# The MLP's first product by seven block products instead of eight, with weight sums made by DMA

## Chip, cores, metric

The kernel runs on one core of a Trainium2 chip, as one program and one launch. The metric is device time in microseconds of that program; lower is better. It was timed in 3 runs, and one more execution was taken with the profiler.

## What is computed

One decoder layer on 512 tokens of width 1024 in f32: retention with 8 heads, native sparse attention with 16 heads, a gated merge of both, an MLP with a squared ReLU, and a gated per-layer embedding. The part that the change touches most:

```
x  = x + (g_ret * o_ret + g_nsa * o_nsa) @ w_out[i]
h2 = rms_norm(x, norm_mlp_g[i])
x  = x + jnp.square(jax.nn.relu(h2 @ w_mlp_up[i])) @ w_mlp_down[i]        # 1024 -> 4096 -> 1024
x  = x + (p[i] @ w_ple_proj[i]) * jax.nn.sigmoid(rms_norm(x, norm_ple_g[i]) @ w_ple_gate[i])
return rms_norm(x, norm_final_g)
```

## The kernel before

Activations lie with features on the 128 partitions and the 512 tokens along the row; a tile is 128 x 512. Every f32 product is made of three matmuls (`mm3`, L254): each operand is split into a rounded part `hi` and a rest `lo`, and hi x hi, hi x lo and lo x hi are added in PSUM. Weights come from DRAM in pieces of 128 x 1024 (512 KB, class `Piece`) on SP's queue, into three buffers `raw`. ScalarE makes `hi` (L206) and VectorE `lo` (L209) of each half of a piece; there are rings of four such halves. In a matmul row of the profile, `ps_s<-gx_hi,hi 128x512` has the moving operand first and the stationary one after it.

The order of work is a list of items, `items`, that `run` (L223) walks through. An item has TensorE's part, a `post` step that takes the result from PSUM, and the weight halves that it needs; behind TensorE's part `run` lists the splits of up to three halves ahead, then what earlier steps put off with `defer`, then `post`. Each engine works through its own instructions in this order, and waits where an operand is not there.

Stages in order of time: norm and the narrow projections; eight retention heads, where the dense projections of head h are listed between the core of head h - 1 (`head_core`, L794; `mixed`, L892), with the output projection `ret_out` (L874) after every second head; sparse attention; the merge; `w_out`; the MLP; the embedding gate; the final norm.

- A head's core ends in a group norm. VectorE makes statistics, POOL runs a chain of 11 small operations for the inverse root (`rsqrt` with `eng=pool`, L302 to L298, result `rs_y`; VectorE for the last head), VectorE scales (`on`, L846), TensorE transposes (L857), VectorE gates.
- The MLP goes in two halves of 16 tiles of 128 hidden features. `up` (L1337) makes one tile: 8 blocks of 128 along the contraction, 24 matmuls of 512 columns, moving `gx`, the gained x. Its `post` multiplies by the norm's factor `rb1`, takes the ReLU, squares it and splits it into `hh` and `hl`. `down` (L1350) adds the second product of that half to `x1`.
- `gained` (L1306) makes `gx_hi` and `gx_lo` and sums squares for the next norm; `token_rstd` and `over_partitions` make the factor and spread it.
- `finish`, `deliver` and `finished` (L1414 to L1487) make the last norm by blocks of 128 tokens: gate with a tanh, add, square with a sum, gain on POOL, inverse root (POOL for two blocks, VectorE for two), multiply, store on SP.

Of the kernel before, what the change touches and what calls it, by code (L numbers as in the profile page):

```python
# [8 lines left out]
F32 = mybir.dt.float32  # L9
# [131 lines left out]
def _layer_kernel(ctx, tc, a, out):  # L141
# [35 lines left out]
    def issue(p):  # L177
        if p.keep:
            if p.raw is None:
                p.raw = P_[p.keep].tile([P, p.n], F32, name=f"raw_{p.keep}_{p.mark}")  # L180
                sp.dma_start(p.raw, p.src)
        elif p.raw is None:
# [3 lines left out]
            sp.dma_start(p.raw, p.src)  # L186
# [67 lines left out]
    def mm3(ps, sh, sl, mh, ml, first, last):  # L254

        pe.matmul(ps, sh, mh, start=first, stop=False)  # L256
        pe.matmul(ps, sh, ml, start=False, stop=False)  # L257
        pe.matmul(ps, sl, mh, start=False, stop=last)  # L258
# [77 lines left out]
    def token_rstd(accs, tag):  # L336


        def sums():
            ps = bank("t")  # L340
# [12 lines left out]
    def over_partitions(tag, dst):  # L353


        def go():
            T["bc"] = bank("t")
# [436 lines left out]
    def head_core(h):  # L794
# [76 lines left out]
        its.append(Item(0.9, turn, gated))  # L871
# [377 lines left out]
    def merge_start():  # L1249
        close("aw", "q", "kv")  # L1250
        T["nsa_p"] = []
        open_("np", bufs=1)
        open_("mp", bufs=1, side="right")
        open_("mw", bufs=2, side="right")
# [41 lines left out]
    def out_start():  # L1296
        close("mw", "np", "oret")
        xp = open_("xp", bufs=1)
        T["x1"] = [xp.tile([P, S], F32, name=f"x1_{n}") for n in range(KT)]
        T["gx"] = [(xp.tile([P, S], F32R, name=f"gx_hi{n}"), xp.tile([P, S], F32R, name=f"gx_lo{n}")) for n in range(KT)]  # L1300
        T["rb1"] = xp.tile([P, S], F32, name="rb1")
        open_("ew", bufs=2)
# [3 lines left out]
    def gained(n, g, acc):  # L1306

        hi, lo = T["gx"][n]
        x = T["x1"][n]
        gc = gains[:, g + n : g + n + 1]  # L1310
        act.activation(hi, x, AF.Copy, scale=gc)
        dve.scalar_tensor_tensor(lo, x, gc, hi.bitcast(F32), op0=ALU.mult, op1=ALU.subtract)
# [8 lines left out]
    for n in range(KT):  # L1321
# [5 lines left out]
        def post_x(ps, n=n):  # L1327
            dve.tensor_tensor(T["x1"][n], ps, T["xs", n], op=ALU.add)
            gained(n, G_MLP, "acc1")
# [4 lines left out]
    gxs = (lambda: T["gx"], KT)  # L1334
    hid = {}

    def up(hf, i):  # L1337
        def post(ps):
            t = P_["ew"].tile([P, S], F32, tag="t1", name="relu")
            dve.scalar_tensor_tensor(t, ps, 0.0, T["rb1"], op0=ALU.max, op1=ALU.mult)  # L1340
            hi = P_["hid"].tile([P, S], F32R, tag=f"hh{i}", name="hh")
            lo = P_["hid"].tile([P, S], F32R, tag=f"hl{i}", name="hl")
            act.activation(hi, t, AF.Square)  # L1343
            dve.tensor_tensor(t, t, t, op=ALU.mult)
            dve.tensor_tensor(lo, t, hi.bitcast(F32), op=ALU.subtract)
            hid[hf, i] = hi, lo

        return dense(("d", "v", "s", "s")[i % 4], [Piece(a["w_mlp_up"][16 * hf + i])], gxs, post)

    def down(hf, n):  # L1350
        def post(ps):
            x = T["x1"][n]
            dve.tensor_tensor(x, ps, x, op=ALU.add)
            if hf == 1:
                gained(n, G_PLE, "acc2")
# [3 lines left out]

    bc = over_partitions("n1", lambda: T["rb1"])  # L1360
    ups = [up(0, i) for i in range(16)]

    posts = []
    for u in ups[:2]:
        posts.append(u[-1].post)
        u[-1].post = None
    def mlp_start():
        close("mp", "th", "nf", "nx", "h")
        fp = open_("fp", bufs=1, side="right")
        T["ppf"] = fp.tile([P, NQ, D], F32, name="pp")  # L1370
# [12 lines left out]
    items += sum(ups[4:], [])
    items += sum((down(0, n) for n in range(KT)), [])
    add(Item(0, load_pp))
    items += sum((up(1, i) for i in range(16)), [])
    items += sum((down(1, n) for n in range(KT)), [])


    def ple_start():  # L1390
        close("hid")
        open_("fw", bufs=1, side="right")
# [5 lines left out]
    def turn_x(t, f2):  # L1398
# [7 lines left out]
        return Item(0.44, go, lambda: dve.tensor_tensor(T["x2t"][:, t, f], T["xt"], T["ppf"][:, t, f], op=ALU.add))  # L1406
# [7 lines left out]
    def finish(t, c0, c1, ps, col):  # L1414

        f = slice(c0, c1)
        x = lambda: T["x2t"][:, t, f]
# [6 lines left out]
        def take():  # L1424
            th = st["th"][:, : c1 - c0]
            dve.tensor_tensor(th, th, T["ppf"][:, t, f], op=ALU.mult)
            dve.tensor_tensor(x(), x(), th, op=ALU.add)

        def square():
            sq = P_["ew"].tile([P, S], F32, tag="sq", name="sq")  # L1430
            act.activation(sq[:, : c1 - c0], x(), AF.Square, accum_out=T["ss2"][:, t, col : col + 1])
            pool.tensor_tensor(x(), x(), T["gf"][:, f], op=ALU.mult)
# [3 lines left out]
    def deliver(t, cols):  # L1436
# [3 lines left out]
        def factors():  # L1440
# [5 lines left out]
            st["r"] = rsqrt(v, 1, "fn", pool if t < NQ - 2 else dve)  # L1446

        def scaled():
            r = st["r"]
            o = P_["fw"].tile([P, D], F32, tag="o", name="o", bufs=4)  # L1450
            act.activation(o[:, 0:S], T["x2t"][:, t, 0:S], AF.Copy, scale=r[:, 0:1])
            dve.tensor_scalar_mul(o[:, S:], T["x2t"][:, t, S:], r[:, 0:1])
# [176 lines left out]
```

## Time and profile before

| | us |
|---|---|
| median of 3 runs | 1268.94 (1268.21 to 1271.06) |
| the profiled execution | 1269.14 |
| its span | 1267.4 |
| TensorE busy | 1245.6 |
| VectorE busy | 770.9 |
| ScalarE busy | 528.8 |
| POOL busy | 213.4 |

The span is what the profile sees from its first to its last instruction; the execution's time is 1.7 us longer. Rows give a start in us, a duration in us, the engine (PE is TensorE, PEld its weight loads, DVE VectorE, ACT ScalarE, POOL GpSimd, SPq the queue that issues loads and stores), the line and the tiles, out<-in. Matmul rows overlap, since they are pipelined: the step from start to start is what one costs.

### The profile page before, as it was taken

The numbers are of one execution on the slowest core, as the hardware profiler recorded it, in microseconds if no ns is written. First come the engines' busy times: TensorE is split into PE (matmuls) and PEld (weight loads), VectorE is DVE, ScalarE is ACT, GpSimd is POOL, SyncE is SP. The second block draws the span as 40 slices with busy tenths as digits, with TensorE's granted clock in tenths as the row PEclk, the third lists the DMA queues.
The fourth block names the chain that finished last, engine by engine and source line by source line (L and its number), as shares of the span: only waits on it lengthen the run. The fifth ranks groups of instructions, "written<-read, shape, count | busy, mean of one in ns | idle before, by whom it ended". The sixth has DMA issues, their size and how long they took to land.

```text
span 1267.4 us, 16784 instructions
## 1 busy us (share of the span) xinstructions
PE 1245.6 (98%) x6312; PEld 1033.0 (82%) x6312; DVE 770.9 (61%) x1401; ACT 528.8 (42%) x1091; POOL 213.4 (17%) x290
## 2 busy tenths in 40 slices
PE   8999999999999999999999999999999999999996
PEld 6968898898998987788888888888888888888885
DVE  6766763665666587778878754555652345644456
ACT  5753333332332233677778642343322223323333
POOL 0040000000000023556574500000000000000045
PEclk9999999999999999999999999999999999999998
DMA  7532323223223222211010033332233342323221
GB/s 248 204 133 67 105 79 100 76 92 100 76 78 98 86 73 84 67 34 35 34 51 17 18 100 100 122 127 91 93 100 100 98 168 86 98 100 100 88 79 67
DMA packets 34513, 116.29 MB, mean 92 GB/s; under 512 B 4096, under 2 KB 4480, under 8 KB 34304
## 3 DMA queue, kind: packets, MB, share of 16 engines
q1 hardware_dynamic: 34432, 115.22, 27.8%
q8 instruction: 50, 0.82, 0.3%
q14 instruction: 31, 0.25, 0.1%
HBM read 111.01 MB, written 4.19 MB: 91 GB/s over the span
## 4 chain that ended last, share of the span: by engine, by line
PE 50%; DVE 2%; POOL 0%; ACT 0%; issue 0%; DVEq 0%; ACTq 0%
PE ps_s L256 6%; PE ps_s L257 6%; PE ps_s L258 6%; PE ps_d L256 4%; PE ps_d L258 4%; PE ps_d L257 4%; PE ps_v L256 3%; PE ps_v L257 3%; PE ps_v L258 3%; PE ps_t L1089 2%; PE ps_t L258 1%; PE ps_t L257 1%; PE ps_t L256 1%; PE ps_v L1106 1%; PE ps_v L1105 1%; PE ps_s L1014 1%
## 5 line engine op out<-in xcount | busy, mean ns | idle before, releaser
L206 ACT ACTIVATE hi<-raw 128x512 fp32r<-128x512 f32 (+1 forms) x364 | 222.7, 622 | 256.4 <-PE ps_v L258 60.5
L209 DVE TENSOR_TENSOR lo<-raw,hi 128x512 fp32r<-128x512 f32 (+1 forms) x350 | 242.5, 715 | 67.7 <-ACT hi L206 67.6
L209 POOL TENSOR_TENSOR lo_fw<-raw_fw,hi_fw 128x512 fp32r<-128x512 f32 x8 | 11.3, 1437 | 503.0 <-ACT hi_fw L206 503.0
L256 PE MATMUL ps_d<-h_hi,hi 128*128 128x512 f32 x216 | 89.6, 415 | 0.0
L258 PE MATMUL ps_d<-h_hi,lo 128*128 128x512 f32 x216 | 85.4, 395 | 0.0
L257 PE MATMUL ps_d<-h_lo,hi 128*128 128x512 f32 x216 | 85.3, 395 | 0.0
L1067 POOL TENSOR_TENSOR pr<-pr,rr 128x512 f32<-128x512 f32 x80 | 84.5, 1087 | 0.0
L1032 ACT ACTIVATE pr<-ps_s,nm 128x128 f32<-128x128 f32 (+3 forms) x128 | 66.0, 525 | 21.5 <-DVE sc L1026 15.5
L256 PE MATMUL ps_t<-h_hi,hi 128*128 128x512 f32 x160 | 64.2, 401 | 0.0
L1098 DVE TENSOR_TENSOR ptl<-ps_t,pth 128x512 fp32r<-128x512 f32 x80 | 53.9, 684 | 16.5 <-ACT pth L1093 14.5
L258 PE MATMUL ps_t<-h_hi,lo 128*128 128x512 f32 x160 | 63.4, 396 | 0.3 <-DVE lo L209 0.3
L257 PE MATMUL ps_t<-h_lo,hi 128*128 128x512 f32 x160 | 63.3, 395 | 0.0
L1024 DVE TENSOR_REDUCE nm<-ps_s 128x2 f32<-128x256 f32 (+3 forms) x64 | 52.1, 815 | 14.3 <-PE ps_s L1017 14.0
L302 POOL TENSOR_TENSOR rs_q<-rs_y 128x4 f32<-128x4 f32 (+1 forms) x9 | 4.4, 491 | 325.9 <-DVE rs_y L292 325.9
L1343 ACT ACTIVATE hh<-relu 128x512 fp32r<-128x512 f32 x32 | 20.3, 634 | 93.5 <-DVE relu L1340 93.5
L1093 ACT ACTIVATE pth<-ps_t 128x512 fp32r<-128x512 f32 x80 | 47.3, 598 | 22.6 <-PE ps_t L1089 18.6
L258 PE MATMUL ps_s<-hh,lo 128*128 128x512 f32 x128 | 50.8, 397 | 0.0
L256 PE MATMUL ps_s<-hh,hi 128*128 128x512 f32 x128 | 50.7, 396 | 0.0
L257 PE MATMUL ps_s<-hl,hi 128*128 128x512 f32 x128 | 50.7, 396 | 0.0
L256 PE MATMUL ps_s<-gx_hi,hi 128*128 128x512 f32 x128 | 50.6, 395 | 0.0
L258 PE MATMUL ps_s<-gx_hi,lo 128*128 128x512 f32 x128 | 50.5, 395 | 0.0
L257 PE MATMUL ps_s<-gx_lo,hi 128*128 128x512 f32 x128 | 50.5, 395 | 0.0
(459 smaller groups left out, 3388.4 us busy)
## 6 DMA issues: line engine op xcount, KB each, us to landing
raw<-in_w_ret_qkg_dram SPq DMA_DIRECT2D x32, 512.0 KB, 3.4
raw<-in_w_mlp_up_dram SPq DMA_DIRECT2D x32, 512.0 KB, 3.7
raw<-in_w_mlp_down_dram SPq DMA_DIRECT2D x32, 512.0 KB, 3.6
raw<-in_w_ret_v_dram SPq DMA_DIRECT2D x16, 512.0 KB, 3.5
raw<-in_w_ret_o_dram SPq DMA_DIRECT2D x16, 512.0 KB, 3.5
raw<-in_w_merge_gate_dram SPq DMA_DIRECT2D x16, 512.0 KB, 3.6
raw<-in_w_nsa_dram SPq DMA_DIRECT2D x12, 512.0 KB, 3.5
o_ret<-in_cmp_w_dram SPq DMA_DIRECT2D x8, 512.0 KB, 5.1
```

The lines of the kernel that those rows point to most:

```text
L206: act.activation(p.hi[i], p.raw[:, c], AF.Copy)
L209: eng.tensor_tensor(p.lo[i], p.raw[:, c], p.hi[i].bitcast(F32), op=ALU.subtract)
L256: pe.matmul(ps, sh, mh, start=first, stop=False)
L257: pe.matmul(ps, sh, ml, start=False, stop=False)
L258: pe.matmul(ps, sl, mh, start=False, stop=last)
L1024: dve.tensor_reduce(self.nm[:, j, :], self.seen(j), axis=AX.XY, op=ALU.max, negate=True)
L1032: act.activation(self.pr[:, j, br, 0 : self.nk].rearrange("p (b j) -> p b j", j=P), self.seen(j)[:, br], AF.Exp, bias=self.nm[:, j, br : b ...
L1067: pool.tensor_tensor(p, p, self.rr[:, :, 1 + br : 2 + br].broadcast_to([P, 4, P]), op=ALU.mult)
L1089: pe.transpose(self.t[i][:, j * P : (j + 1) * P], self.pr[:, j, br, kb * P : (kb + 1) * P], ident)
L1093: act.activation(hi, self.t[i], AF.Copy)
L1098: dve.tensor_tensor(lo, self.t[i], self.pt[i][0].bitcast(F32), op=ALU.subtract)
L1343: act.activation(hi, t, AF.Square)
```

## The change

The contraction (1024) is cut into halves j, the 512 tokens into two halves, and two tiles of 128 hidden features, i = 0 and 1, make one of 16 pairs q. Of such a 2 x 2 by 2 x 2 block product, seven block products are made in place of eight (class `UpPair`), each with 4 blocks of 128 along the contraction, moving 256 columns: 84 matmuls of 256 columns per pair for 48 of 512. The seven combinations of x (`x00`, `x10`, `x11`, `t1` to `t4`) are made once in the `w_out` stage, in `gained`, now with the argument `seven` and put off with `defer`. The four sums of weight blocks (`s1` to `s4`, 4 MB each) lie in DRAM. They are made by 64 DMAs of 512 KB on POOL's queue, some plain, some adding to what lies there (`sum_steps`), listed among the items of heads 1 to 7 (`among`). In the MLP a piece is then loaded as two blocks of 128 x 512, from the weights or from the sums. The rows of i = 1 come out negated, so their ReLU takes the minimum. The norm's factor leaves the first product; the second product is multiplied by its square, `rb2`. Some closing steps are listed anew: all inverse roots of the last norm on VectorE, the last quarter's gain in VectorE's last multiply, one store on ACT's queue. The last head's gating is listed ahead of the look-ahead splits.

```diff
+    def load(self, sp):
+        if isinstance(self.src, list):
+            for i, x in enumerate(self.src):
+                w = self.n // len(self.src)
+                sp.dma_start(self.raw[:, i * w : (i + 1) * w], x)
...
+    w_up = a["w_mlp_up"].rearrange("(q i) k (j c) -> i j q k c", i=2, j=2)
+    sums = {x: dram.tile([16, P, S], F32, name=f"sum_{x}") for x in ("s1", "s2", "s3", "s4")}
+    def sum_steps(q):
...
+        todo = [("s1", w(1, 1), False), ("s3", w(0, 0), False), ("s1", w(1, 0), True), ("s3", w(1, 0), True), ("s2", w(0, 0), False), ("s2", t["s1"], True), ("s4", w(0, 1), False), ("s4", t["s2"], True)]
+        return [lambda x=x, src=src, add_=add_: pool.dma_start(t[x], src, **(dict(accum_op=ALU.add, max_dma_last_dim=4 * S) if add_ else {})) for x, src, add_ in todo]
...
-        its.append(Item(0.9, turn, gated))
+        its.append(Item(0.9, turn, gated, eager=h == NH - 1))
...
+    folds_ = sum((sum_steps(slice(i, i + 2)) for i in range(0, 16, 2)), [])
...
     for h in range(1, NH):
-        its = mixed(head_dense(h), head_core(h - 1))
+        its = among(mixed(head_dense(h), head_core(h - 1)), folds_[64 * (h - 1) // 7 : 64 * h // 7])
...
+    def taken(x, k, v, sign=1.0):
+        hi, lo = seventh(x, k)
+        act.activation(hi, v, AF.Copy, scale=sign)
+        if sign == 1.0:
+            defer(lambda: dve.tensor_tensor(lo, v, hi.bitcast(F32), op=ALU.subtract))
...
+        pool.tensor_tensor(d, d, t[:, H:], op=ALU.add)
+        pool.tensor_tensor(t0[:, H:], t[:, H:], t0[:, H:], op=ALU.subtract)
+        pool.tensor_tensor(t0[:, :H], d, t[:, :H], op=ALU.subtract)
...
+        def product(self, name, piece, col):
+            ps_, x, first = {"p5": ("b", "t1", True), "m1": ("a", "x00", True), "m2": ("c", "x10", True), "p6": ("a", "t2", False), "p3": ("b", "x11", False),
+                             "p7": ("a", "t3", False), "p4": ("a", "t4", False)}[name]
...
+                for k in range(4):
+                    mm3(ps, *piece.cols(col + k * P, col + k * P + P), *seventh(x, k), first and k == 0, k == 3, not first)
...
+        def after_p5(self):
+            act.activation(self.s5, self.b, AF.Copy)
+        def after_m1(self):
+            act.activation(self.s[:, :H], self.a, AF.Copy)
+        def after_m2(self):
+            dve.tensor_tensor(self.r0[:, :H], self.c, self.s[:, :H], op=ALU.add)
+        def after_p6(self):
+            act.activation(self.s[:, H:], self.a, AF.Copy)
+        def after_p3(self):
+            dve.tensor_tensor(self.r0[:, H:], self.b, self.s[:, H:], op=ALU.add)
+            self.squares(0, self.r0)
+        def after_p7(self):
+            dve.tensor_tensor(self.r1[:, H:], self.a, self.s5, op=ALU.add)
+        def after_p4(self):
+            dve.tensor_copy(self.r1[:, :H], self.a)
+            self.squares(1, self.r1)
...
+            dve.scalar_tensor_tensor(t, t, 0.0, t, op0=ALU.min if i else ALU.max, op1=ALU.mult)
+            act.activation(hi, t, AF.Copy)
+            defer(lambda: dve.tensor_tensor(lo, t, hi.bitcast(F32), op=ALU.subtract))
...
+        order_ = [("p5", 0), ("m1", 0), ("p5", 1), ("m1", 1), ("m2", 0)]
+        for i in range(6):
+            order_ += [("p6", i)] + [("m1", i + 1)] * (i > 0) + [("p3", i), ("p7", i), ("p5", i + 2), ("m2", i + 1), ("p4", i)]
...
-            dve.tensor_tensor(x, ps, x, op=ALU.add)
+            dve.tensor_tensor(t, ps, T["rb2"], op=ALU.mult)
+            dve.tensor_tensor(x, x, t, op=ALU.add)
...
-            st["r"] = rsqrt(v, 1, "fn", pool if t < NQ - 2 else dve)
+            st["r"] = rsqrt(v, 1, "fn")
```

Three places where the order of instructions differs. First POOL between the inverse roots of the retention heads 0 and 1. Before, the last operation for head 0 is followed at once by the first for head 1:

```order
L297 TENSOR_SCALAR rs_q<-rs_q 128x4
L298 TENSOR_TENSOR rs_y<-rs_q,rs_y 128x4
L302 TENSOR_TENSOR rs_q<-rs_y 128x4
L303 TENSOR_TENSOR rs_q<-rs_q,ve 128x4
L304 TENSOR_SCALAR rs_r<-rs_q 128x4
```

Now (the same operations carry the line numbers of the changed file, and the sums are numbered 80 to 83):

```order
L306 TENSOR_TENSOR rs_y_1332<-rs_q_1333,rs_y_1332 128x4
L355 DMA sum_s2_81<-in_w_mlp_up_dram 256x1x512
L355 DMA sum_s2_81<-sum_s1_80 256x512
L355 DMA sum_s4_83<-in_w_mlp_up_dram 256x1x512
L355 DMA sum_s4_83<-sum_s2_81 256x512
L355 DMA sum_s1_80<-in_w_mlp_up_dram 256x1x512
L355 DMA sum_s3_82<-in_w_mlp_up_dram 256x1x512
L355 DMA sum_s1_80<-in_w_mlp_up_dram 256x1x512
L355 DMA sum_s3_82<-in_w_mlp_up_dram 256x1x512
L355 DMA sum_s2_81<-in_w_mlp_up_dram 256x1x512
L310 TENSOR_TENSOR rs_q_1760<-rs_y_1759 128x4
```

Nine transfers stand ahead of the chain of head 1; a transfer that reads or adds to a sum waits for the landing of the one that wrote it.

Second, VectorE in the first product of the MLP. Before, three rows follow each tile's product, and two splits:

```order
L1340 SCALAR_TENSOR_TENSOR relu<-ps_v,rb_8181 128x512
L1344 TENSOR_TENSOR relu<-relu 128x512
L1345 TENSOR_TENSOR hl<-relu,hh 128x512
L209 TENSOR_TENSOR lo<-raw,hi 128x512 x2
L1340 SCALAR_TENSOR_TENSOR relu<-ps_s,rb_8181 128x512
```

Now, for one pair:

```order
L1468 TENSOR_TENSOR r_10685<-ps_t,s_10562 128x256
L1484 SCALAR_TENSOR_TENSOR r_10685<-r_10685 128x512
L217 TENSOR_TENSOR lo<-raw,hi 128x512
L1486 TENSOR_TENSOR hl<-r_10685,hh 128x512
L1473 TENSOR_TENSOR r_10789<-ps_v,s_10540 128x256
L217 TENSOR_TENSOR lo<-raw,hi 128x512 x2
L1462 TENSOR_TENSOR r_10830<-ps_s,s_10746 128x256
L217 TENSOR_TENSOR lo<-raw,hi 128x512
L1476 COPY r_10789<-ps_v 128x256
L1484 SCALAR_TENSOR_TENSOR r_10789<-r_10789 128x512
L217 TENSOR_TENSOR lo<-raw,hi 128x512
L1486 TENSOR_TENSOR hl<-r_10789,hh 128x512
```

Every weight block of 512 columns is split as before, but a pair has seven of them where it had four; the products are taken in four operations of 256 columns (`r` is a pair's result, `s` a copied product).

Third, VectorE at the end. Before:

```order
L1426 TENSOR_TENSOR pth<-pth,pp 128x256
L1427 TENSOR_TENSOR x2t<-x2t,pth 128x256
L1452 TENSOR_SCALAR o<-x2t,rs_y 128x512 x2
L1443 TENSOR_SCALAR fv<-ss_8539 128x1
L1445 SCALAR_TENSOR_TENSOR fv<-ss_8539,fv 128x1 x2
```

Now:

```order
L1627 TENSOR_SCALAR o<-x2t,rs_y 128x512
L1592 TENSOR_TENSOR pth<-pth,ppx 128x256
L1593 TENSOR_TENSOR x2t<-x2t,pth 128x256
L1610 TENSOR_SCALAR fv<-ss_8684 128x1
L1612 SCALAR_TENSOR_TENSOR fv<-ss_8684,fv 128x1 x2
```

The two multiplications of 512 columns that stood between the last addition and the last sum of squares are gone from there; one of them now stands ahead of the last addition.

## Rows read from the trace of the kernel before

**Rows 1.** The page's first part: busy time, share of the span, instructions.
```profile
span 1267.4 us, 16784 instructions
...
PE 1245.6 (98%) x6312; PEld 1033.0 (82%) x6312; DVE 770.9 (61%) x1401; ACT 528.8 (42%) x1091; POOL 213.4 (17%) x290
```

**Rows 2.** What TensorE waited for: us in total, times, longest.
```profile
PE ps_d L257 <- DVE rtl L868: 1.0, 2, 0.7
...
PE ps_d L256 <- ACT rth L867: 0.3, 1, 0.3
```

**Rows 3.** TensorE's timeline: first matmul of `up`'s second half, and of the `down` behind it.
```profile
1026.87 0.39 PE L256 MATMUL ps_d<-gx_hi,hi 128*128 128x512 f32 x1
...
1116.47 0.40 PE L256 MATMUL ps_d<-hh,hi 128*128 128x512 f32 x1
```

**Rows 4.** TensorE's timeline in a head's value projection, matmuls of 256 columns.
```profile
329.87 0.28 PE L256 MATMUL ps_d<-hi,h_hi 128*128 128x256 f32 x1
...
334.94 0.28 PE L257 MATMUL ps_v<-lo,h_hi 128*128 128x256 f32 x1
```

**Rows 5.** Busy time by stretch; after POOL: granted clock, DMA share, GB/s.
```profile
329.00:335.00 6.00, 6.00 (x53) 6.00 (x52) 2.64 (x11) 0.63 (x1) 2.06 (x9) 1.00 0.21 42
...
800.00:830.00 30.00, 30.00 (x130) 24.14 (x129) 16.38 (x25) 11.41 (x20) 0.00 (x0) 1.00 0.45 144
...
890.00:950.00 60.00, 60.00 (x259) 48.57 (x258) 33.39 (x52) 18.14 (x31) 0.00 (x0) 1.00 0.30 97
...
1000.00:1010.00 10.00, 10.00 (x44) 8.03 (x43) 2.67 (x5) 1.93 (x4) 0.00 (x0) 1.00 0.32 105
```

**Rows 6.** Timeline (two rows), then instructions grouped by form: busy us, mean ns.
```profile
878.48 1.29 DVE L209 TENSOR_TENSOR lo<-raw,hi 128x512 fp32r<-128x512 f32 x2
...
120.41 0.62 DVE L317 TENSOR_TENSOR inl<-inn,inh 128x256 fp32r<-128x256 f32 x2
...
L317 DVE TENSOR_TENSOR inl<-inn,inh 128x256 fp32r<-128x256 f32 x8 | 3.3, 418 | 0.0
...
L206 ACT ACTIVATE hi<-raw 128x512 fp32r<-128x512 f32 x356 | 219.5, 626 | 256.4 <-PE ps_v L258 60.5 <-PE ps_d L257 53.4 <-PE ps_s L257 52.9
...
L1432 POOL TENSOR_TENSOR x2t<-x2t,gf 128x256 f32<-128x256 f32 x2 | 1.8, 902 | 0.0
```

**Rows 7.** DMA issues (KB each, median us to landing); the first stretch's busy times.
```profile
raw<-in_w_ret_qkg_dram SPq DMA_DIRECT2D x32, 512.0 KB, 3.4
raw<-in_w_mlp_up_dram SPq DMA_DIRECT2D x32, 512.0 KB, 3.7
...
0.00:31.70 31.70, 25.85 (x126) 21.27 (x127) 21.79 (x42) 18.77 (x34) 1.73 (x9) 1.00 0.70 248
```

**Rows 8.** POOL's timeline: end of a chain, and the two next chains' first operations.
```profile
130.57 0.20 POOL L298 TENSOR_TENSOR rs_y<-rs_q,rs_y 128x4 f32<-128x4 f32 x1
167.32 0.57 POOL L302 TENSOR_TENSOR rs_q<-rs_y 128x4 f32<-128x4 f32 x1 [36.55 <-DVE rs_y L292]
...
229.77 0.57 POOL L302 TENSOR_TENSOR rs_q<-rs_y 128x4 f32<-128x4 f32 x1 [58.98 <-DVE rs_y L292]
```

**Rows 9.** Timeline of VectorE and of TensorE behind the first chain.
```profile
130.81 1.90 DVE L846 TENSOR_SCALAR on<-ps_s,mv,rs_y 128x256 f32<-128x256 f32 x4 [3.03 <-POOL rs_y L298]
...
133.36 1.04 PE L857 MATMUL ps_s<-cst,on 128*128 128x128 f32 x8
```

**Rows 10.** Timeline of the last 12 us: ScalarE and VectorE.
```profile
1255.80 0.47 ACT L1422 ACTIVATE pth<-ps_s,rh 128x256 f32<-128x256 f32 x1 [1.73 <-PE ps_s L258]
...
1258.12 2.33 DVE L1452 TENSOR_SCALAR o<-x2t,rs_y 128x512 f32<-128x512 f32 x2
...
1260.62 0.69 DVE L1445 SCALAR_TENSOR_TENSOR fv<-ss,fv 128x1 f32<-128x1 f32 x2
...
1263.08 0.72 ACT L1451 ACTIVATE o<-x2t,rs_y 128x512 f32<-128x512 f32 x1 [3.22 <-DVE rs_y L300]
```

More of the change, by code (lines that the diff above doesn't have):

```diff
@@ L252, in run, with mm3 @@
                 it.post()
[L254 to L258, printed above, removed]
+    def mm3(ps, sh, sl, mh, ml, first, last, again=False):
+        pe.matmul(ps, sh, mh, start=first, stop=False, skip_group_check=again)
+        pe.matmul(ps, sh, ml, start=False, stop=False, skip_group_check=again)
+        pe.matmul(ps, sl, mh, start=False, stop=last, skip_group_check=again)
     def dense(tag, pieces, xs, post, nsub=2, off=0):
@@ L1306, in gained @@
[L1306 to L1312 removed]
+        T["rb2"] = xp.tile([P, S], F32, name="rb2")
+        T["gt"] = {}
+        for k in range(KT // 2):
+            for i in range(4):
+                T["gt"][i, k] = [xp.tile([P, S], F32R, tag=f"gt{x}{i}{k}", name="gt") for x in "hl"]
@@ L1313, in gained @@
+    def gained(n, g, acc, seven=False):
+        x = T["x1"][n]
+        if seven:
+            combined(n, g)
+        else:
+            hi, lo = T["gx"][n]
+            gc = gains[:, g + n : g + n + 1]
+            act.activation(hi, x, AF.Copy, scale=gc)
+            dve.scalar_tensor_tensor(lo, x, gc, hi.bitcast(F32), op0=ALU.mult, op1=ALU.subtract)
         if n == 0:
@@ new lines, in load_pp, with x2, pp @@
+        T["pp8"] = [xp.tile([P, S], F32R, tag=free[8 + i], name="ppx").bitcast(F32) for i in range(8)]
+        for i in range(8):
+            sp.dma_start(T["pp8"][i], pp_dram[:, i // 2, i % 2 * S : i % 2 * S + S])
+        sp.dma_start(T["gf"], a["norm_final_g"].broadcast_to([P, D]))
+    def x2(t, c0, c1):
+        i = c0 // S
+        return T["x2"][2 * t + i][:, c0 - i * S : c1 - i * S]
+    def pp(t, c0, c1):
+        i = c0 // S
+        return T["pp8"][2 * t + i][:, c0 - i * S : c1 - i * S]
@@ L1390, in ple_start @@
+    dn = [down(1, n) for n in range(KT)]
+    items += dn[0] + [Item(0, load_pp)] + sum(dn[1:], [])
     def ple_start():
         close("hid")
-        open_("fw", bufs=1, side="right")
+        open_("fw", bufs=1)
         for p in w_pg[1]:
@@ L1482, in _layer_kernel @@
     items += weave(first[16:], turns[4:])
-    behind, late, last = [], [], [(), ()]
-    def finished(steps, ends=(), turn=True):
-        gate_, take, square = steps
-        behind.extend([gate_, *late[:1], take, *(last.pop(0) if turn else ()), *late[1:]])
-        late[:] = [square, *ends[:1]]
-        last.append(ends[1:])
+    behind = []
+    f_ = [finish(t, 0, S, lambda t=t: pw[0, t], 0) for t in range(NQ)]
+    behind.append(f_[0][0])
     for t in range(NQ):
-        finished(finish(t, 0, S, lambda t=t: pw[0, t], 0))
+        behind.extend([*(f_[t + 1][:1] if t + 1 < NQ else ()), *f_[t][1:]])
     banks = iter("ttdvs")
+    scaled = []
     for t in range(NQ):
@@ L1510, in _layer_kernel @@
                         add(Item(0, None, behind.pop(0)))
-            ends = deliver(t, 2 + (t == NQ - 1)) if c1 == S else ()
-            finished(finish(t, S + c0, S + c1, lambda t=t, c0=c0, n=c1 - c0: pw[1, t, c0][:, :n], 1 + (c0 > 0)), ends, t < NQ - 1 or c0 > 0)
-    items += [Item(0, None, f) for f in [*behind, late[0], *last[0], late[1], *last[2]]]
+            gate_, take, square = finish(t, S + c0, S + c1, lambda t=t, c0=c0, n=c1 - c0: pw[1, t, c0][:, :n], 1 + (c0 > 0), c0 == 0)
+            if t == NQ - 1 and c0 == 0:
+                behind.extend([gate_, take])
+                held = square
+                continue
+            behind.extend([gate_, *scaled, held, take, square] if t == NQ - 1 else [gate_, take, *scaled, square])
+            factors, last_ = deliver(t, 2 + (t == NQ - 1))
+            behind.append(factors)
+            scaled = [last_]
+    items += [Item(0, None, f) for f in [*behind, *scaled]]
     run(items)
```

170 lines of the change are left out of this document (118 added, 52 removed).

## The prediction

> **What bounds the kernel now.** Three views, in this order. The busy table first: TensorE is busy 1245.6 us of a span of 1267.4 [rows 1], so 21.8 us are all that other work can ever cost it. The list of what TensorE waited for comes next: outside the first load the long entries are about a microsecond, two of them before the last retention output projection (1.0 us on `rtl`, 0.3 us on `rth`) [rows 2]. Third the timeline and the table by stretch around the MLP: in 890 to 950 us TensorE has work for 60.00 of 60 us, VectorE for 33.39 and ScalarE for 18.14 [rows 5]. So the MLP's first product goes at TensorE's own pace, and what is taken from TensorE there comes off the end as long as nothing else grows past it.
>
> **What one matmul costs.** The second half of the first product runs from 1026.87 to 1116.47 us [rows 3]: 89.60 us for 16 tiles of 24 matmuls, 384 in all, so 0.2333 us for 512 columns. The two halves hold 768, 179.2 us. The changed kernel has 16 pairs x 7 products x 4 blocks x 3 matmuls = 1344 of 256 columns. That form is in the kernel already: in the value projection of a head 44 matmuls of 256 columns begin between 329.87 and 334.94 us, 43 steps, 0.1179 us each [rows 4], at the full granted clock. The weight loads fill that stretch entirely (6.00 of 6.00 us, against 8.03 of 10.00 with 512 columns) [rows 5], yet the step is within 1% of half of 0.2333, so a load for every 256 columns still costs next to nothing. 1344 x 0.1179 = 158.5 us. **First term: -20.7 us.** One eighth of 179.2 would be 22.4; the rest goes to overhead of shorter matmuls. I take the row.
>
> **Does anything else grow past TensorE there?** One pair takes TensorE 84 x 0.1179 = 9.90 us. VectorE has per pair 7 `lo` subtractions and 4 operations on 512 columns, and 4 on 256. A row of 512 lasts 0.69 us, but two that do not wait for each other begin 0.60 apart (1.29 us for two) [rows 6]; for 256 columns it is 0.42 and 0.31 (0.62 for two) [rows 6]. So 11 x 0.60 + 4 x 0.31 = 7.8 us at best and 11 x 0.69 + 4 x 0.42 = 9.3 us at worst, 79 to 94% of 9.90. It was 56% before. ScalarE has 12 operations per pair, 7.5 us if each costs the 0.626 us of a 512 row [rows 6]. Both fit, VectorE with 0.6 to 2.1 us to spare. Parts of weights live in rings of four and last 1.41 us each on TensorE, so a `lo` has some 4 us from the time its buffer is free: the chain ScalarE then VectorE takes 1.3 us plus what stands ahead. Two places are tighter: the bank of `p5` of the next but one pair is free only when VectorE has read `p3`, with one product (1.41 us) between, and the same holds for `m1` behind `p4`. VectorE reads first thing (0.42 us), so I price both at nothing; without that cover each would cost some tenths of a microsecond per pair. Loads: 512 KB per 2.83 us is 185 GB/s, now as two transfers; 248 GB/s were moved at a share of 0.70 [rows 7], and a load lands in 3.7 us [rows 7], against some 5.7 us that three buffers leave. Free, but near.
>
> Around the start of the stage there are three POOL operations of 0.90 us [rows 6] behind the last output-projection tile, and a chain of ten small VectorE operations for the norm; the first four products need neither. **Stalls there: 0 to 4 us; I take 2**, the middle, since VectorE's spare time is small.
>
> **DMA sums on POOL's queue.** 64 transfers of 512 KB go on a queue that now holds, in this stretch, only the 11 operations per head that end in `rs_y`. POOL takes them in order: behind each chain nine transfers, then the next chain. From the end of one chain to the call for the next are 36.55 or 58.98 us, in turn [rows 8]. VectorE waits at `on` for `rs_y` (3.03 us, from 127.8 to 130.81), and TensorE's transposes begin at 133.36, only 0.65 us after `on` is done (130.81 + 1.90) [rows 9]: whatever POOL is late beyond that, TensorE stands still. The trace of before has no transfer issued by POOL. Bounds: as a load of 512 KB that SP issues, 3.4 to 3.7 us [rows 7]; then even nine transfers one behind the other are 33 us and fit. In a short gap three waits lie in a row (`s2` before its sum, `s4` before its sum, the next `s1` before its sum), so the last of nine is issued after three landings and some issue time, and lateness begins at about 10 to 12 us a landing. At the other end a transfer could be carried by two of the 16 engines (its source is a view whose outer extent is two): 248 / 0.70 / 16 = 22.1 GB/s for one engine, 524 KB / 2 / 22.1 = 11.9 us. The likeliest value is nearer the SP row, since it is the same size between the same memory and the same engines: I take **no cost**. SP's own loads in the heads have three buffers, each of 24 x 0.2333 = 5.6 us of TensorE work, and bear a landing some microseconds longer.
>
> **The rest.** Last head's `gated` step now precedes the look-ahead splits: at most the 1.3 us of [rows 2], **-1.3**. The tail: the last product's result is taken at 1255.80 and the last multiply ends at 1263.08 + 0.72, 8.0 us [rows 10]. In it VectorE multiplies two blocks of 512 for 2.33 us beside POOL, before it turns to the last sum of squares, whose chain is 1260.62 to 1263.08 [rows 10]. Now one such block stays ahead, POOL has no chain, and VectorE ends the last quarter itself: 0.47 (the take) + 0.6 (one multiply) + 2 x 0.42 + 0.6 (the square and its sum) + 2.5 (the chain) + 0.72 = 5.7, and 6.2 with some contention from POOL. **-1.8**, between 0 and -2.5. The second product's extra 16 multiplications (0.69 us each) stand beside 11 us of TensorE work each, the squared norm factor replaces the plain one: nothing. The output-projection stage gives VectorE three operations of 256 columns more in four tiles and five in the other four, and takes one of 512 away: at most 5 x 0.42 - 0.69 = 1.4 us in a tile of 5.6, where it was busy 16.38 of 30 us [rows 5]: covered.
>
> **Sum**, against the profiled execution's 1269.14 us (span 1267.4; it lies 0.02% above the median of 1268.94): 1269.1 - 20.7 + 2.0 - 1.3 - 1.8 = **1247.3 us**.
>
> **Rivals.**
> *A transfer takes 12 us* (copies and additions of weights on two engines, sums of sums on all). Stepping the nine of the first short gap: `s2` lands at 12.9, its sum is issued at 13.9, `s4` lands at 26.8, its sum is issued at 27.8, the next `s1` lands at 40.7, and the ninth transfer is issued at 43 to 44 us where the chain is called at 36.55. Late by 7, 6.3 us of it on TensorE, in three short gaps: 19 us, and 1266. For it: the source's outer extent, and nothing of before that shows otherwise. Against it: at 9.5 us a landing the same steps end in time. The Trainium skill, "DMA: Bandwidth & Descriptors", section on why a DMA increments its semaphore by 16, says that the engine count is the largest number up to 16 that divides the slowest dimension of both sides; here these are 2 and 256, so it says two engines, with an exception for some direct copies from this queue. By that rule this rival is the forecast; no run here shows it yet.
> *Slower than before:* the same place, but an addition, which also reads what it adds to, takes twice as long, 24 us. Then sums wait for additions in the long gaps too: stepping all six gaps I get 7, 13, 17, 4, 17 and 0 us late, 55 us of TensorE standing, 1302 us. It decides from about 13 us per landing in the chain, where the lateness outgrows the 22 us gained.
> *The stage stays as long as VectorE lets it:* in-order waits on products add about 0.6 us to VectorE's 9.3 per pair, 0.5 to 1 us per pair on TensorE, 16 pairs: 1257. For it the 94%; against it the two-at-a-time rows.
>
> **How the numbers follow.** Forecast 0.52; VectorE or loads 0.16; POOL late by some microseconds 0.20; POOL late by much 0.12. Low end: no stalls and the tail at -2.5 gives 1244.6, less a little: 1243. High end 1267 takes in the second rival and leaves out the 0.12 and a piece of the neighbours. Within 0.2% is about what a measurement of this kernel can tell, 2.5 us either way: faster is the first two and half of the third, 0.78; same 0.08; slower 0.14.
>
> **What would show it.** Right: 1344 steps of 0.118 us in two stages of about 80 us each, TensorE without waits in the heads, `on` released 3 us after VectorE asks, last multiply about 6 us after the last matmul. Wrong: idle TensorE before the transposes of heads 1, 3 and 5 with `rs_y` as releaser (POOL), or idle time before products of the first MLP product with `lo` or a DMA as releaser.

## The result, and the profile after

The changed kernel takes 1446.1 us (median of 4 runs, 1445.37 to 1446.74) where the kernel before took 1269.57 beside it: a ratio of 1.139, 95% interval 1.137 to 1.141. Forecast was 1247.3, and the range ended at 1267: wrong in sign and by 199 us. The profiled execution took 1446.74 us. The page's first part, its line of granted clock and its two lines on the new queue:

```profile
span 1444.9 us, 18634 instructions
...
PE 1240.8 (86%) x6888; PEld 1056.7 (73%) x6888; DVE 826.5 (57%) x1538; ACT 577.6 (40%) x1215; POOL 297.1 (21%) x343
...
PEclk9999979696997879878999999999999999999999
...
q0 software_dynamic: 70656, 34.02, 12.1%
...
sum_s<-in_w_mlp_up_dram POOLq DMA_DIRECT2D x48, 512.0 KB, 20.4
```

TensorE is busy about as long as before [rows 1], but 204 us of the span are now idle, where it was 21.8. The list of waits says for what (us in total, times, longest; `issue` in place of a releaser means that the profile shows nothing that the engine waited for):

```profile
POOL sum_s L355 <- DMA sum_s<-in_w_mlp_up_dram: 337.1, 18, 31.4
DVE on L867 <- POOL rs_y L306: 178.8, 7, 37.9
...
PE ps_s L878 <- DVE on L867: 145.7, 6, 32.9
...
POOL sum_s L355 <- issue: 108.0, 10, 18.5
...
PE ps_s L264 <- ACT inh L324: 35.1, 1, 35.1
```

Read from the bottom: TensorE stands 35.1 + 145.7 = 180.8 us, in seven places; `on` stands for POOL's `rs_y`, 178.8 us in place of the 3.03 us a head of [rows 9]; and POOL stands 337.1 + 108.0 = 445 us for landings of its own transfers. (A landing is the time from a transfer's listing until its bytes lie in DRAM. Of the 108.0 under `issue`, 107.4 are seven waits of 13.1 to 18.6 us ahead of the last sum of a group, right behind the listing of the copy that it adds to, so they count as landings here.) In the timeline, one such chain, that of head 1:

```profile
146.59 0.96 POOL L355 DMA_DIRECT2D sum_s<-sum_s  x1 [14.90 <-DMA sum_s<-in_w_mlp_up_dram]
147.20 1.47 POOL L355 DMA_DIRECT2D sum_s<-in_w_mlp_up_dram  x1
165.88 0.90 POOL L355 DMA_DIRECT2D sum_s<-sum_s  x1 [17.21 <-DMA sum_s<-in_w_mlp_up_dram]
166.47 2.48 POOL L355 DMA_DIRECT2D sum_s<-in_w_mlp_up_dram  x2
183.90 4.93 POOL L355 DMA_DIRECT2D sum_s<-in_w_mlp_up_dram  x3 [14.96 <-DMA sum_s<-in_w_mlp_up_dram]
187.16 1.89 POOL L310 TENSOR_TENSOR rs_q<-rs_y 128x4 f32<-128x4 f32 x1
...
191.99 1.90 DVE L867 TENSOR_SCALAR on<-ps_s,mv,rs_y 128x256 f32<-128x256 f32 x4 [24.12 <-POOL rs_y L306]
...
192.68 1.95 PE L878 MATMUL ps_s<-cst,on 128*128 128x128 f32 x8 [19.27 <-DVE on L867]
...
217.92 0.95 POOL L355 DMA_DIRECT2D sum_s<-sum_s  x1 [25.96 <-DMA sum_s<-in_w_mlp_up_dram]
...
238.57 0.91 POOL L355 DMA_DIRECT2D sum_s<-sum_s  x1 [18.55 <-issue]
```

A copy listed at 147.20 is on the ground at 165.88, when the addition behind it may start: some 18 us. The additions listed from 183.90 on release the next sum at 217.92: some 33 us. Eight transfers, for two pairs, make a group. From the last addition of one group (165.88) to that of the next (238.57) are 72.7 us, and over the seven such steps up to the last, at 655.26, 69.9 in the mean. Eight groups are 559 us of POOL's time. From POOL's first transfer, at 89.9, to the first operation that sparse attention wants of it (460.76 in the trace before) are 371. The difference, 188, is what TensorE stands, within 8 us.

The seventh place has another path. POOL begins sparse attention behind its last transfer, 195 us later than the 460.76; ScalarE has stood 41.63 us for that operation, and the `inh` that TensorE wants is listed behind it on ScalarE:

```profile
655.88 1.58 POOL L964 TENSOR_TENSOR nr<-nr,nr 128x512 f32<-128x512 f32 x1
...
657.49 1.28 ACT L971 ACTIVATE qcat<-nr 64x512 fp32r<-64x512 f32 x2 [41.63 <-POOL nr L964]
658.79 1.04 ACT L324 ACTIVATE inh<-inn 128x512 fp32r<-128x512 f32 x2
```

The rest of the loss is the granted clock. Three stretches (busy times of PE, PEld, DVE, ACT, POOL; then the clock, the DMA share, GB/s): the stall, what follows it, and later:

```profile
173.40:192.60 19.20, 0.01 (x1) 0.00 (x0) 0.61 (x2) 0.60 (x1) 7.21 (x14) 0.55 0.31 68
192.70:200.00 7.30, 7.30 (x29) 5.86 (x30) 7.30 (x13) 2.31 (x4) 0.00 (x0) 0.78 0.61 155
200.00:215.00 15.00, 15.00 (x66) 12.06 (x65) 10.71 (x17) 5.02 (x10) 0.00 (x0) 1.00 0.55 151
```

While TensorE has nothing to do the granted clock falls toward the lower of its two levels (1.2 of 2.4 GHz), and the 7.3 us after the wait run at a mean of 0.78, which costs 7.3 x 0.22 = 1.6 us. The seven stretches of 7.2 to 7.7 us behind the seven stalls had 0.62 to 0.79: 14.6 us together. 180.8 + 14.6 = 195.4; and 1446.1 less that is 1250.7, which the first run below measured to within 0.3 us.

The closing steps gained less than their term. In the timeline, from the last product's taking to the last multiply's end are 1440.60 + 0.48 - 1434.20 = 6.9 us, 8.0 before [rows 10]:

```profile
1434.20 0.47 ACT L1588 ACTIVATE pth<-ps_s,rh 128x256 f32<-128x256 f32 x1 [1.75 <-PE ps_s L266]
...
1440.60 0.48 DVE L1625 SCALAR_TENSOR_TENSOR o<-x2t,rs_y,gf 128x256 f32<-128x256 f32 x1
```

### The profile page after: what moved, and what is told of

Read it like the earlier page. It is cut to its first block, busy times and chain, and to the rows that moved or that the text cites. A ratio compares the mean times of both kernels' runs of the same rounds, so it can differ in the third digit from the quotient of the medians.

```text
span 1444.9 us, 18634 instructions
## 1 busy us (share of the span) xinstructions
PE 1240.8 (86%) x6888; PEld 1056.7 (73%) x6888; DVE 826.5 (57%) x1538; ACT 577.6 (40%) x1215; POOL 297.1 (21%) x343
## 3 DMA queue, kind: packets, MB, share of 16 engines
q0 software_dynamic: 70656, 34.02, 12.1%
## 5 line engine op out<-in xcount | busy, mean ns | idle before, releaser
L214 ACT ACTIVATE hi<-raw 128x512 fp32r<-128x512 f32 (+1 forms) x412 | 250.1, 621 | 236.4 <-PE ps_v L266 60.5
L217 DVE TENSOR_TENSOR lo<-raw,hi 128x512 fp32r<-128x512 f32 (+1 forms) x398 | 279.2, 716 | 58.3 <-ACT hi L214 57.9
L878 PE MATMUL ps_s<-cst,on 128*128 128x128 f32 x64 | 13.8, 388 | 145.7 <-DVE on L867 145.7
L878 PEld LDWEIGHTS ps_s<-cst,on 128*128 128x128 f32 x64 | 9.1, 189 | 149.1 <-issue 146.7
L867 DVE TENSOR_SCALAR on<-ps_s,mv,rs_y 128x256 f32<-128x256 f32 x32 | 15.2, 538 | 178.8 <-POOL rs_y L306 178.8
L355 POOL DMA_DIRECT2D sum_s<-in_w_mlp_up_dram x48 | 70.0, 1700 | 118.0 <-DMA sum_s<-in_w_mlp_up_dram 117.1
L355 POOL DMA_DIRECT2D sum_s<-sum_s x16 | 14.9, 929 | 327.5 <-DMA sum_s<-in_w_mlp_up_dram 220.1
L888 ACT ACTIVATE rth<-gated 128x512 fp32r<-128x512 f32 x16 | 10.0, 631 | 169.5 <-DVE gated L885 169.3
L264 PE MATMUL ps_t<-h_hi,hi 128*128 128x512 f32 x160 | 67.6, 422 | 0.0
L264 PE MATMUL ps_s<-vh,inh 128*128 128x256 f32 x80 | 23.5, 294 | 35.1 <-ACT inh L324 35.1
## 6 DMA issues: line engine op xcount, KB each, us to landing
sum_s<-in_w_mlp_up_dram POOLq DMA_DIRECT2D x48, 512.0 KB, 20.4
```

What stands on the lines that cost most here:

```text
L214: act.activation(p.hi[i], p.raw[:, c], AF.Copy)
L217: eng.tensor_tensor(p.lo[i], p.raw[:, c], p.hi[i].bitcast(F32), op=ALU.subtract)
L264: pe.matmul(ps, sh, mh, start=first, stop=False, skip_group_check=again)
L355: return [lambda x=x, src=src, add_=add_: pool.dma_start(t[x], src, **(dict(accum_op=ALU.add, max_dma_last_dim=4 * S) if add_ else {})) fo ...
```

## Experiments

Theory: a transfer whose source has an outer extent of two is carried by two of the 16 engines and lands late; POOL, which works in order, waits for such landings ahead of its chains. Rivals: the additions are slow whatever carries them; the bytes crowd the memory; only the chains' place behind the transfers costs; the seven products lose time themselves.

**Rows outermost (e1_rows_outer).** Same transfers, bytes and waits:

```diff
-        w = lambda i, j: w_up[i, j, q]
-        t = {x: t[q] for x, t in sums.items()}
+        w = lambda i, j: w_up[i, j, q].rearrange("q k c -> k q c")
+        t = {x: t[q].rearrange("q k c -> k q c") for x, t in sums.items()}
```

> The same 64 transfers with the same bytes and the same waits, but both sides listed with the 128 rows outermost instead of the two pairs. Theory (a transfer whose source has an outer extent of 2 is carried by two engines; POOL, which waits for landings in order, is then late for its chain): the median landing of the transfers from the weights falls from 20.4 us to 4 to 7 us, POOL's waits for landings fall from 445 us to under 150, TensorE's waits for `on` (145.7) and for `inh` (35.1) fall under 5 in all, and the time is 1251 us (1248 to 1256), the 477.4 + 771.8 + 1.8 of heads as before and the rest as after. Rival, an adding transfer is slow by itself whatever carries it: adding ones stay near 20 us and the time over 1350. Rival, bytes between DRAM and DRAM crowd everything: no change, 1440.

Measured: 1250.91 us (1250.51 to 1251.46), ratio 0.9855 (0.9838 to 0.9871) to the kernel before. From its page, then its waits:

```profile
q0 software_dynamic: 13312, 33.56, 11.5%
...
sum_s<-in_w_mlp_up_dram POOLq DMA_DIRECT2D x48, 512.0 KB, 8.2
```

```profile
POOL sum_s L355 <- DMA sum_s<-in_w_mlp_up_dram: 106.2, 18, 11.5
...
POOL sum_s L355 <- issue: 34.7, 8, 7.2
...
DVE on L867 <- POOL rs_y L306: 21.0, 7, 3.0
```

The landing is 8.2 where I said 4 to 7, POOL's waits are 141 us in place of 445, and `on` waits 3.0 us a head, as before the change. TensorE's waits for `on` and for `inh` are gone from its list. Two lines on how a view is listed give back 195 us, and this version beats both kernels.

The packets show how many engines there were. The same bytes take 70656 packets in the change and 13312 here. Counted by size, the difference is 57344 packets of 8 bytes, too small to carry the weights. If each idle engine gets as many of them as a working engine has data packets (64 of 4096 bytes for a copy, 128 of 2048 for an addition), this is (32 copies x 64 + 16 additions x 128) x 14: it comes out for two engines at work and for no other number. The Trainium skill's rule, in "DMA: Bandwidth & Descriptors", section on why a DMA increments its semaphore by 16, that the engines are the largest number up to 16 that divides the slowest dimension of both sides, holds here, and in the next two kinds of transfer.

**Four and eight pairs in a transfer (e2_four_pairs, e6_eight_pairs).** Outer extent 4 and 8, same bytes in all:

```diff
-    folds_ = sum((sum_steps(slice(i, i + 2)) for i in range(0, 16, 2)), [])
+    folds_ = sum((sum_steps(slice(i, i + 4)) for i in range(0, 16, 4)), [])
...
-        its = among(mixed(head_dense(h), head_core(h - 1)), folds_[64 * (h - 1) // 7 : 64 * h // 7])
+        its = among(mixed(head_dense(h), head_core(h - 1)), folds_[32 * (h - 1) // 7 : 32 * h // 7])
```

With 8 and 16 in place of 4 and 32 this is the second run.

> 32 transfers of 1 MB in place of 64 of 512 KB: the source's outer extent is 4, the bytes are the same. Theory of the engines: four carry one transfer, so twice the bytes still land in about 20 us each, POOL has half the landings to wait for (about 220 us in place of 445), is late by 0 to 10 us in the short gaps alone, and the time is 1251 to 1280. Rival, the bytes set it: a landing takes about 40 us and the time stays near 1440.

> 16 transfers of 2 MB: outer extent 8. Theory: eight engines carry one transfer, so four times the bytes of the change land in the same 17 us (copy) or 33 us (addition); POOL has 16 landings in place of 64, two groups of about 70 us, and at most two or three of them in a gap: in time or up to 10 us late once or twice, 1251 to 1270. Rival, bytes set the landing: four times 17 and 33 us, POOL as late as in the change, 1440.

Measured: 1282.17 and 1252.5 us (one run each). The pages' lines, of the four and then of the eight:

```profile
q0 software_dynamic: 37376, 33.75, 11.9%
...
sum_s<-in_w_mlp_up_dram POOLq DMA_DIRECT2D x24, 1024.0 KB, 26.6
```

```profile
q0 software_dynamic: 20736, 33.62, 11.3%
...
sum_s<-in_w_mlp_up_dram POOLq DMA_DIRECT2D x12, 2048.0 KB, 28.5
```

Two and four times the bytes land in 26.6 and 28.5 us for 20.4, 1.3 and 1.4 times as long: it is mainly the share of one engine that counts, not the bytes. The 8-byte packets are 24576 = (16 x 64 + 8 x 128) x 12 and 8192 = (8 x 64 + 4 x 128) x 8, so 4 and 8 engines. With four, TensorE still waited twice for `on` (24.3 us), more than the 0 to 10 I allowed in a gap, and the time lies 2 us above the range given; with eight it no longer waited for it.

**No sums (e3_no_sums).** No transfers; the products read blocks of weights:

```diff
-    folds_ = sum((sum_steps(slice(i, i + 2)) for i in range(0, 16, 2)), [])
+    folds_ = []
...
-            self.w = {"m1": w_up[0, 0, q], "m2": w_up[0, 1, q], "p4": w_up[1, 1, q], "p5": sums["s1"][q], "p6": sums["s2"][q], "p7": sums["s3"][q], "p3": sums["s4"][q]}
+            self.w = {"m1": w_up[0, 0, q], "m2": w_up[0, 1, q], "p4": w_up[1, 1, q], "p5": w_up[1, 1, q], "p6": w_up[0, 0, q], "p7": w_up[1, 0, q], "p3": w_up[0, 1, q]}
```

> No transfers on POOL's queue; where the products read a sum, they read a block of the weights of the same size (the sums are left out of what is computed). Theory: all of the loss lies in the transfers, so heads as before and the rest as after: 477.4 + 771.8 + 1.8 = 1251 us (1248 to 1253), against 1247.3 forecast. Rival, the seven products or the re-listed steps lose time themselves: over 1260.

Measured: 1251.08 us (1249.36 to 1252.18), ratio 0.9853 (0.9839 to 0.9868). All of the loss lies in the transfers, and with 16 engines they cost nothing that the times show: this and the first run are the same.

**Chains on VectorE (e4_chain_dve).**

```diff
-            rs = rsqrt(ve, NQ, "gn", pool if h < NH - 1 else dve)
+            rs = rsqrt(ve, NQ, "gn")
```

> The transfers as in the change, but the inverse roots of all heads on VectorE, so that no head waits for POOL. Theory (POOL's queue as a whole is too long, some 515 us of landings from 90 us on, not only badly placed beside the chains): TensorE has no wait for `on`, but POOL's first operation of the sparse attention, due at about 461 us, comes at 590 to 625, and TensorE stands for 120 to 160 us there: 1370 to 1415 us. Rival, only the place of the chains behind the transfers costs: 1251 to 1260.

Measured: 1431.66 us (one run), above the range: seven stalls became one. Its timeline and its waits:

```profile
640.76 0.90 POOL L355 DMA_DIRECT2D sum_s<-sum_s  x1 [15.26 <-issue]
641.73 1.26 POOL L964 TENSOR_TENSOR nr<-nr,nr 128x512 f32<-128x512 f32 x1
```

```profile
PE ps_s L264 <- ACT inh L324: 177.5, 1, 177.5
```

POOL comes to sparse attention at 641.73, 181 us after the 460.76 of before. I had set 515 us for its transfers; eight groups of 69.9 are 559. So the place of the chains is not the cause: POOL's whole list is too long. Moving the chains elsewhere saves 14.4 us, 3.3 of TensorE's standing and the rest about the clock behind six stalls.

**No landing to wait for (e5_no_waits).** Two engines still, but each of the 64 a copy to a place of its own:

```diff
-        todo = [("s1", w(1, 1), False), ("s3", w(0, 0), False), ("s1", w(1, 0), True), ("s3", w(1, 0), True), ("s2", w(0, 0), False), ("s2", t["s1"], True), ("s4", w(0, 1), False), ("s4", t["s2"], True)]
+        todo = [("s1", w(1, 1), False), ("s3", w(0, 0), False), ("s5", w(1, 0), False), ("s7", w(1, 0), False), ("s2", w(0, 0), False), ("s6", w(1, 1), False), ("s4", w(0, 1), False), ("s8", w(0, 1), False)]
```

> 64 transfers of 512 KB, all from the weights with the outer extent of 2, but none adds and none reads a sum: each goes to a place of its own in DRAM, so POOL has no landing to wait for (the sums are left out of what is computed). Theory (it is the waiting in POOL's order that costs, not the transfers beside the loads): POOL only issues, nine by 1.2 to 1.6 us in a gap, is in time for every chain, TensorE's waits for `on` are under 3 us, the landings stay at 15 us or more, and the time is 1250 to 1257. Rival, slow transfers on two engines hold up the weight loads that use the same engines: loads land late and TensorE waits for `hi` or `lo`, 1270 or more.

Measured: 1251.79 us (one run), with landings of 18.4 us. Slow copies that nobody waits for cost nothing that this run shows; loads of `w_ret_qkg` beside them landed in 4.7 us where it was 3.4 [rows 7], and no wait of TensorE came of it. But POOL did not only issue. It stood 58.6 us although no transfer waits for another, six times for 8.5 to 9.4 us behind seven copies; no chain was late by it:

```profile
POOL sum_s L355 <- issue: 58.6, 12, 9.4
...
233.24 7.48 POOL L355 DMA_DIRECT2D sum_s<-in_w_mlp_up_dram  x7
249.22 1.06 POOL L355 DMA_DIRECT2D sum_s<-in_w_mlp_up_dram  x1 [8.49 <-issue]
```

**Additions alone, copies alone on 16 engines (e10_adds_wide, e11_copies_wide).**

```diff
+        r = lambda v, k_outer: v.rearrange("q k c -> k q c") if k_outer else v
-        return [lambda x=x, src=src, add_=add_: pool.dma_start(t[x], src, **(dict(accum_op=ALU.add, max_dma_last_dim=4 * S) if add_ else {})) for x, src, add_ in todo]
+        return [lambda x=x, src=src, add_=add_: pool.dma_start(r(t[x], add_), r(src, add_), **(dict(accum_op=ALU.add, max_dma_last_dim=4 * S) if add_ else {})) for x, src, add_ in todo]
```

In the second, `not add_` stands for the `add_` in `r`.

> Rows outermost for the additions only; the copies keep the outer extent of 2. Of the three landings that POOL waits for in a row in a group (copy, addition, copy; 69.9 us a group in the change: some 17 + 33 + 17 and the issuing), the middle one becomes 14 as in the first run: 49 us a group, 8 x 49 = 392 against 371 from the first transfer to POOL's first operation of the sparse attention: 21 us too many in all, and some more by short gaps: 1270 to 1300. Rival, the additions are the whole trouble: 1251.

> Rows outermost for the copies only; the additions keep the outer extent of 2 where they read the weights. 7 + 33 + 7 and the issuing: 48 us a group, 8 x 48 = 384 against 371: 13 us too many in all, and some more by short gaps: 1265 to 1300. Rival, the additions are the whole trouble: near the change's 1446.

Measured: 1383.28 and 1310.13 us (one run each), both above their ranges. A group takes 60.6 and 53.5 us by the same rows as above (last additions at 167.13 to 591.51, and at 144.10 to 518.85). In the first I had two copies in the row; there are three, since the second sum's copy is listed behind the additions and lands after them: 18 + 20 + 20 and the issuing. In the second the two copies took 6.5 and 10.6 us (189.68 to 196.23 and 196.82 to 207.39), and the chains in between came on top. The arithmetic holds with the measured groups: 8 x 60.6 - 371 = 114, and TensorE stands 89.5 + 28.6 = 118; 8 x 53.5 - 371 = 57, and it stands 30.5 + 17.9 = 48. Neither kind of transfer is the whole trouble: each costs time on two engines.

**The waits put far apart (e9_relisted, e12_wide_relisted).** Copies first, then additions; the second also with rows outermost:

```diff
-    folds_ = sum((sum_steps(slice(i, i + 2)) for i in range(0, 16, 2)), [])
+    by_ = [sum_steps(slice(i, i + 2)) for i in range(0, 16, 2)]
+    folds_ = [g[j] for js in ((0, 1, 4, 6), (2, 3), (5,), (7,)) for g in by_ for j in js]
```

> The change's 64 transfers, with the outer extent of 2 and so two engines each, and the same sums; only their order on POOL's queue is another: the 32 copies first, then the 16 additions from the weights, then the 8 sums of sums for the second sum, then the 8 for the fourth, so that what a transfer waits for landed long ago. Theory (the loss is slow landings times waits in POOL's order): POOL's waits for landings fall from 445 us to under 60, no wait for `on` over 3 us, 1250 to 1257 us. Rival, the slow landings alone make POOL late: 1300 or more.

> The order of the run e9_relisted (copies first, then additions, then the sums of sums) and rows outermost on both sides as in e1_rows_outer. Theory (what held POOL in e9_relisted, under the name issue, is a queue that takes no more transfers while slow ones are under way, so slow additions hold it even where nothing waits for a landing): with 16 engines each, POOL's waits under the name issue fall from 137.8 us to under 40, waits for landings under 25, no wait for `on` over 3.1 us, and the time is that of e1_rows_outer, 1249 to 1253. Rival, listing many additions together fills the queue whatever carries them: POOL late again in the gaps of heads 4 and 5, 1270 or more.

Measured: 1295.59 us (1294.64 to 1297.28), ratio 1.0208 (1.0191 to 1.0225), and 1251.03 (1249.4 to 1253.58), ratio 0.9851 (0.9834 to 0.9869). The first is a miss. Its waits:

```profile
POOL sum_s L355 <- issue: 137.8, 18, 25.9
...
DVE on L867 <- POOL rs_y L306: 66.2, 7, 42.0
...
PE ps_s L878 <- DVE on L867: 41.1, 2, 36.9
...
POOL sum_s L355 <- DMA sum_s<-in_w_mlp_up_dram: 17.6, 2, 17.3
```

and its timeline where the additions begin:

```profile
272.74 6.94 POOL L355 DMA_DIRECT2D sum_s<-in_w_mlp_up_dram  x4
305.61 1.88 POOL L355 DMA_DIRECT2D sum_s<-in_w_mlp_up_dram  x1 [25.94 <-issue]
307.74 1.88 POOL L355 DMA_DIRECT2D sum_s<-in_w_mlp_up_dram  x1 [0.24 <-issue]
311.34 1.87 POOL L355 DMA_DIRECT2D sum_s<-in_w_mlp_up_dram  x1 [1.73 <-issue]
334.02 1.87 POOL L355 DMA_DIRECT2D sum_s<-in_w_mlp_up_dram  x1 [20.80 <-issue]
```

The waits for landings fell as expected, to 17.6 and another 5.2 us for sums of sums, and POOL was late all the same, once by enough to hold TensorE 36.9 us; the 41.1 us of both times are most of the 44.6 us between this run and the next. POOL stands between transfers that wait for nothing the profile shows: 25.9 us after the first four additions, then 12.7 to 20.8 us after every third. The fifth addition starts 32.9 us after the first, about the time that one takes to land. Copies show the same, as in e5_no_waits: 8.7 to 9.0 us after seven of them. So POOL's queue seems to take only so many slow transfers at once. With 16 engines the same order has no such wait (0.2 us at POOL's transfers in all) and the time of the first run. My theory in its first form, that only waits for landings cost, does not hold; a slow landing holds POOL in two ways, and 16 engines end both. That it is a limit of the queue is read from these waits and from their going; no run counted its places.

**The small terms (e7_no_eager, e8_old_tail).** On the first run's kernel, the gating listed late again, and the closing steps as before:

```diff
-        its.append(Item(0.9, turn, gated, eager=h == NH - 1))
+        its.append(Item(0.9, turn, gated, eager=False))
```

```diff
-            st["r"] = rsqrt(v, 1, "fn")
+            st["r"] = rsqrt(v, 1, "fn", pool if t < NQ - 2 else dve)
...
-            behind.extend([gate_, *scaled, held, take, square] if t == NQ - 1 else [gate_, take, *scaled, square])
+            finished(finish(t, S + c0, S + c1, lambda t=t, c0=c0, n=c1 - c0: pw[1, t, c0][:, :n], 1 + (c0 > 0)), ends, t < NQ - 1 or c0 > 0)
```

> The kernel of the first run (rows outermost) with the last head's gating listed behind the look-ahead splits again, as before. The forecast's term would make it 1.3 us longer (1252.2). The trace of the first run still shows the waits for `rtl` (0.9) and `rth` (0.3), so I expect no difference over 0.3 us: 1250.9.

> The kernel of the first run with the closing steps listed as before (POOL's chains and gains, both 512-column multiplications ahead of the last sum of squares). From the traces, the last product's taking to the last multiply's end is 6.84 us in the first run and 8.0 before; so 1.2 us longer: 1252.1. The forecast's term was 1.8.

Measured: 1252.06 us (1250.8 to 1253.67), ratio 0.9866 (0.985 to 0.9883), and 1253.46 (1251.36 to 1254.16), ratio 0.9872 (0.9858 to 0.9887). Both intervals overlap that of the first run (0.9838 to 0.9871), so the times can't decide. The traces do. TensorE's wait for `rtl` is the same with the gating early and late; the first run, then the run without:

```profile
PE ps_d L265 <- DVE rtl L889: 0.9, 2, 0.7
```

```profile
PE ps_d L265 <- DVE rtl L889: 1.0, 2, 0.7
```

And the old tail takes 1244.76 + 0.49 - 1237.43 = 7.8 us from the last taking to the last multiply, against 6.9 in the first run.

## Why the prediction was wrong, step by step

- **The step that failed** is the price of a transfer on POOL's queue: "The likeliest value is nearer the SP row ... I take **no cost**". A load of SP's queue, 3.4 to 3.7 us, stood for transfers with another shape of view, and the cost was 195 us. The bound at the other end, two engines, was in the text with its reason, and the runs showed it: landings of some 18 us for a copy and 33 for an addition.
- **The rival was priced low too.** Two engines stood at 12 us (1266) and an addition at 24 (1302). The 12 had the bytes on two engines and nothing else; in the trace an engine has its 64 packets done in 64 x 0.166 = 10.6 us, yet the sum behind the copy starts 18 us after the copy's listing. An addition's 128 packets of 0.19 us are 24 us, and 33 pass. What fills the rest was not pursued. The stepping itself was right where the landings are: with 16 to 19 us each in the first short gap, the chain of head 1 begins at 187.16 where it was called at 167.32 before [rows 8], and TensorE stands 19.27.
- **The end of POOL's list was not looked at.** The stepping stopped at the last gap between chains. Lateness that a gap doesn't take back goes on to sparse attention: eight groups of three landings in a row, held against the 371 us of room, give the loss within 8 us with the measured 69.9 a group. With the 12 and 24 of the slower rival the same sum is (12 + 24 + 12 + 3) x 8 = 408, 37 over the room; that is less than the 55 of its stepping, so it would not have made the rival dearer, but it points at POOL's first operation of sparse attention (35.1 us here), which the prediction did not name.
- **A stall's second price**, the clock behind it, was not in the sum: 14.6 us for seven.
- **Right:** that TensorE has next to no slack against POOL at the transposes, so that POOL's lateness stops it; and which place to look at, `rs_y` ahead of `on`.
- **The first product** was sized well, seen in the first run's timeline, where nothing else disturbs it (first and last of the second half's 672 steps, and the next product):

```profile
1018.98 0.28 PE L264 MATMUL ps_t<-gt,hi 128*128 128x256 f32 x1
...
1098.84 0.28 PE L266 MATMUL ps_v<-gt,lo 128*128 128x256 f32 x1
1098.95 0.39 PE L264 MATMUL ps_d<-hh,hi 128*128 128x512 f32 x1
```

  79.97 us for 672 matmuls are 0.1190 a step (0.1179 forecast), where it was 89.60 [rows 3]: -9.6. The first half, with the stalls at its start, went from 91.0 to 83.5: -7.5. Together -17.1 against -20.7 + 2.0 = -18.7.
- **VectorE stayed behind TensorE**: 8.80 of 10 us in the stretch 1030 to 1040 of that run, inside the 79 to 94% worked out, and TensorE is busy all of it: that rival fell.
- **The gate of the last head** gave nothing of the -1.3. The wait for `rtl` did not come from the splits ahead of it, as I took it to; what sets it was not pursued.
- **The tail** gave -0.9 to -1.1 of -1.8.

-17.1, 0 and -1.1 are -18.2; the first run is 18.6 below the kernel before. Had the transfers cost nothing, as assumed, the forecast would have been 3.6 us off.

## What to carry to other kernels

Before a transfer on POOL's queue is given a price, look at the outermost extent of both its sides: in the runs here it set how many engines carry it, and listing 128 rows outermost in place of two blocks was worth 195 us. When transfers share an in-order queue with small work that others wait for, sum all the landings that wait for each other over the whole stretch and hold the sum against the room there is, beside stepping through single gaps. Putting the waits far apart is not enough while the transfers are slow: 64 slow copies that nobody waits for cost nothing (e5_no_waits), but slow additions listed one behind the other held POOL and cost 44.6 us (e9_relisted).

## What was not expected of the hardware

- Engines that a POOL transfer leaves out are, by the count, not left alone: each got an 8-byte packet for every packet of a working one (57344 of the 70656 packets in the change, none with rows outermost).
- An addition costs an engine more than a copy of the same bytes: a packet of 2048 bytes took 0.19 us, one of 4096 bytes of a copy 0.166 (means in the change's trace).
- POOL stands without a wait that the profile names once some slow transfers are under way (137.8 us in e9_relisted, 58.6 in e5_no_waits where no transfer waits for another, none in e12_wide_relisted with 16 engines).
